# Quarter sums of the down-projection weights: made on VectorE and stored, or made in DRAM by copies and adding DMAs

## The chip, the cores and the metric

The kernel runs on one core of a Trainium2 chip. The metric is the device time of one execution in microseconds (us). Engines are named as in the profile: PE is TensorE (matmuls), PEld its weight loads, DVE is VectorE, ACT is ScalarE, POOL is GpSimd, SP is SyncE, which issues most DMAs here. DMAs that add to their destination are issued from POOL.

## The reference

It is a trunk of two layers over 512 tokens of width 1024, all in float32. Layer 0 mixes tokens with dilated banded attention in three head groups, layer 1 with forgetting attention over shared keys and values. After each mixer comes the same feed-forward part, which is where the change lies:

```python
def conv_ffn(xn, w_up, cw, cb, w_down):
    a = xn @ w_up                                   # 512x1024 @ 1024x5632
    T = a.shape[1]
    ap = jnp.pad(a, ((0, 0), (CONV_W - 1, 0), (0, 0)))
    a = sum(ap[:, j:j + T] * cw[j] for j in range(CONV_W)) + cb
    gate, val = jnp.split(a, 2, axis=-1)
    return (jax.nn.gelu(gate, approximate=True) * val) @ w_down   # 512x2816 @ 2816x1024
```

## The kernel before

Every product in float32 is made of three matmuls on high and low parts (`mm3`, L262): a float32 operand is cast to a rounded high part by ACT, and DVE subtracts that from the original to get the low part. Weights pass through the class `Weights` in a fixed list of pieces of 128 x 1024: `load` issues the DMA on SP (L46) into a tile `wraw` of the pool `t4` (10 buffers), `high` casts it on ACT (L54) into a tile of the pool `t8` (16 buffers), `low` subtracts on DVE (L62). `low_added` (L77) lets an adding DMA on POOL do that subtraction inside the core, from a negated copy that ACT makes; it is used at a few places. Tiles of a pool are handed out in turn, and whoever writes a tile first waits until the readers of its last use are done. The order of the instructions on each engine is the order in which the program writes them; nothing is reordered.

The feed-forward part of a layer (`ffn`) has two phases.

The up-projection runs over NF = 22 chunks `c` of 128 gate channels and the 128 value channels that belong to them. Chunks 6, 8, ..., 18 (`SEVEN`) use a scheme of seven products in place of eight (Strassen's, in Winograd's form); their weight sums are made by `seven_weights`, whose first DVE instructions are L656 and L657. While chunk `c` is multiplied, the weights of chunk `c + 2` are prepared and those of `c + 3` are loaded. `taps`, `glu` and `product` make the convolution, the gate and the product `hc`, and POOL stores `hc` to DRAM (`hD`, L608).

The down-projection (`down`) also uses seven products in place of eight, over ND = 11 pairs `j` of chunks. For it each pair of weight chunks needs sums of quarters. With the pair's two chunks of 128 rows, top and low, each cut into a left and a right half of 512 columns, the four sums are

- T1 = top right - top left, T3 = low right - top right, T2 = low right - T1, and a fourth, low left - T2.

`down_sums` makes them for a list of pairs: SP loads the two chunks (L553 to L555), DVE does four subtractions of 128 x 512 (L558 to L561), and the result is stored to the DRAM tensor `dT[l][j]` (L566), from where `Weights` loads it later as pieces of the down-projection, and `load_two` its last quarter. It is a generator, and each `next` on it takes one step: a load, and a sum and a store that lag behind. The places of these steps are written out by hand:

- during layer 0's attention, ten pairs of layer 0 in tiles of the pool `t8`, stored from SP, and two pairs of layer 1 in `t4`;
- during the projection of the shared keys and values, six pairs of layer 1, in `t4`, stored from POOL;
- at the end of each up-projection (from chunk NF - 3), the layer's last pair of layer 0 or 1 and one more of layer 1, in `t8`, stored from POOL.

On the activation side `pair_sums` makes the matching sums of token halves, and `combine_one` combines the partial products in the matmul banks.

Of the kernel before, what the change touches and what calls it, by code (L numbers as in the profile page):

```python
# [20 lines left out]
NF = DFF // 128  # L21
# [75 lines left out]
def trunk_kernel(ctx, tc, x, norm_gains, w_qkv_a, w_o_a, w_q_b, w_o_b, kv_norm, w_kvf, b_f,  # L97
# [11 lines left out]
    def t8(shape, dt=F32, name="t8"):  # L109
        return p8.tile(shape, dt, tag="t8", name=name)  # L110
# [429 lines left out]
        dve.tensor_copy(cp, pc)  # L540
        return cp

    def down_sums(pairs, place, queue, lag, behind):


        live, n = [], len(pairs)
        for i in range(n + lag + behind):
            if i < n:
                l, j = pairs[i]
                a, b = place()  # L550
                live.append((a, b))
                r = w_down[l][j * 256:j * 256 + 256, :].rearrange("(c p) d -> c p d", p=128)
                sp.dma_start(a, r[0])  # L553
                sp.dma_start(b[:, 0:512], r[1, :, 512:1024])
                sp.dma_start(b[:, 512:1024], r[1, :, 0:512])  # L555
            if 0 <= i - lag < n:
                a, b = live[i - lag]
                dve.tensor_tensor(a[:, 0:512], a[:, 512:1024], a[:, 0:512], ALU.subtract)  # L558
                dve.tensor_tensor(a[:, 512:1024], b[:, 0:512], a[:, 512:1024], ALU.subtract)
                dve.tensor_tensor(b[:, 0:512], b[:, 0:512], a[:, 0:512], ALU.subtract)  # L560
                dve.tensor_tensor(b[:, 512:1024], b[:, 512:1024], b[:, 0:512], ALU.subtract)  # L561
            i -= lag + behind
            if i >= 0:
                l, j = pairs[i]
                for q, t in enumerate(live[i]):
                    queue.dma_start(dT[l][j, :, q * 1024:q * 1024 + 1024], t)  # L566
            yield

    def in_one():
        t = t8([128, 2, 1024], name="dsums")  # L570
        return t[:, 0], t[:, 1]

    def in_two():
        return [t4([128, 1024], name="dsums") for _ in range(2)]

    def ffn(l, bd, cp, nxt, ahead):
        hD = tc.dram_tile([NF, 128, T], F32, name="hD")
# [117 lines left out]
        def pair_sums(j):  # L702

            pair_load(j + 1)
            k = acts[j]
            dve.tensor_tensor(k[:, s3_], k[:, a11], k[:, s1_], ALU.subtract)
            dve.tensor_tensor(k[:, s1_], k[:, s1_], k[:, s2_], ALU.add)
            dve.tensor_tensor(k[:, s2_], k[:, s1_], k[:, a11], ALU.subtract)
            pool.dma_start(sD[j], k[:, s2_])

        def pair_highs(j):
# [52 lines left out]
        def combine_one(bp):  # L764
            a, b, c, d = db[bp, 0], db[bp, 1], db[bp + 2, 0], db[bp + 2, 1]
            p1, u, u3 = (t2([128, 512], name="dsum") for _ in range(3))
            act.copy(p1, a)
            dve.tensor_tensor(u, b, p1, ALU.add)
            dve.tensor_tensor(c, c, u, ALU.add)
            act.copy(u3, c)  # L770
            dve.tensor_tensor(b, d, u, ALU.add)
            dve.tensor_tensor(d, d, u3, ALU.add)


        def p_11(j, bp):
# [98 lines left out]
        extra = sums_in()  # L874
        begun = None
        before = None
        for c in range(2, NF):
            if c == NF - 4:
                pair_load(0)
            if c == NF - 3:  # L880
                sums = down_sums([(l, ND - 1), (1, 8 + l)], in_one, pool, 1, 0)
                next(sums)
            steps = weights(c + 2) if c + 2 < NF else iter(())
            banks = [bank([128, T], name="up") for _ in range(2)]
            if c in SEVEN:
                w = halves.pop(c)
                W.n_get += 2
                x11, x21, x22 = [(xT[0][i], xT[1][i], s) for i, s in ((0, LO), (1, LO), (1, HI))]
                o1, o2, o3, o4 = banks[0][:, LO], banks[0][:, HI], banks[1][:, LO], banks[1][:, HI]
                s1, s12, s17 = (t2([128, 256], name="csum") for _ in range(3))  # L890

                def prod(o, a, x, start=False):
                    half_mm(o, w[a], x[0:2], x[2], start)

                prod(o1, "A11", x11, True)
                prod(o2, "S2", (*XB, HI))
                prod(o3, "S3", (*XA, HI), True)
                product()
                bb = taps(*before)
                act.copy(s1, o1)  # L900
                next(steps)
                dve.tensor_tensor(s12, o2, s1, ALU.add)
                dve.tensor_tensor(s17, o3, s1, ALU.add)
                glu(before[0], bb)
                prod(o1, "A12", x21)
                prod(o2, "S1", (*XA, LO))
                prod(o3, "A22", (*XB, LO))
                next(steps)
                next(steps, None)
                dve.tensor_tensor(o4, o2, s17, ALU.add)  # L910
                begun = W.get(), bank([128, T], name="up")
                up(*begun, range(4))
                prod(o2, "S4", x22)
                next(steps, None)
                dve.tensor_tensor(o3, o3, s12, ALU.add)
                next(steps, None)
                dve.tensor_tensor(o2, o2, s1, ALU.add)  # L917
            else:
                for s in range(2):
                    if s == 0 and begun:  # L920
                        w, banks[0] = begun
                        up(*begun, range(4, KD))
                        begun = None
                    else:
                        up(W.get(), banks[s], range(KD))
                    if c == NF - 2:
                        next(sums)
                    if s == 0 and before:
                        post(*before, (lambda: pair_lows(0)) if c == NF - 1 else None)
                        if c >= NF - 2:  # L930
                            pair_highs(c - NF + 2)
                            pair_sums(c - NF + 3)
                    next(steps, None)
                    next(extra, None)
            run(steps)
            before = c, banks
            if c == NF - 3:
                pair_sums(0)
# [249 lines left out]
    W.ahead = 4  # L1188
    W.split(6)
    qk_post(0, 3, qk_banks[3])  # L1190
    sums = down_sums([(1, 6), (1, 7)], in_two, sp, 1, 3)
    next(sums)
    reorder(2, 3)

    def wide_proj(g, name, post, between):

        banks = [bank([128, T], name=name) for _ in range(4)]
        for s in range(4):
            w = W.get()
            wh, wl = (t.rearrange("p (k c) -> p k c", k=2) for t in w)  # L1200
            for b in range(4):
                for k in range(2):
                    kc = 2 * s + k
                    ah, al = ax(g, b, kc)
                    mm3(banks[b], ah, al, wh[:, k, :], wl[:, k, :], kc == 0, kc == KD - 1)
                if s == 3:
                    post(g, b, banks[b])
            for f in between[s]:
                f()
            next(down0)  # L1210

    def v_post(g, b, o):
        if b == 0:
            for i in (1, 2):
# [1 line left out]
        act.copy(V[1][:, b, :], o[:, 0:256])  # L1216
        dve.tensor_copy(V[2][:, b, :], o[:, 256:512])

    down0 = down_sums([(0, j) for j in range(10)], in_one, sp, 1, 1)
    v_proj0([[L(qk_transpose, 0, 0), L(qk_transpose, 0, 1)],  # L1220
             [L(qk_transpose, 0, 2), L(qk_transpose, 0, 3), L(scores, 0, 0), L(scores, 0, 1), L(next, sums)]])
    wide_proj(1, "qk_ps", qk_post, [
        [L(p_transpose, 0, 0)],
        [L(scores, 0, 2), L(scores, 0, 3), L(p_transpose, 0, 1), L(next, sums)],
        [L(p_transpose, 0, 2), L(next, sums)],
        [stat_out, L(p_transpose, 0, 3), L(next, sums)]])
    wide_proj(2, "qk_ps", qk_post, [
        [L(qk_transpose, 1, 0), L(qk_transpose, 1, 1), L(next, sums)],
        [L(qk_transpose, 1, 2), L(scores, 1, 0), L(scores, 1, 1)],
        [L(qk_transpose, 1, 3), L(p_transpose, 1, 0)],  # L1230
        [L(scores, 1, 2), L(scores, 1, 3), L(p_transpose, 1, 1), stat_in]])
# [125 lines left out]
            Vt[hf] = t8([128, 4, 512], name=f"Vt{hf}")  # L1357
        (act.copy if b % 2 else dve.tensor_copy)(Vt[hf][:, b, :], o)

    down1 = down_sums([(1, j) for j in range(6)], in_two, pool, 1, 0)  # L1360
    first, second = bd2.order[:2], bd2.order[2:]
    bd2.norm(second[1])
    gate = gates()
# [17 lines left out]
            for bb in (first[second.index(blocks[0])], blocks[0]):  # L1381
                keep_values(0, bb, banks[bb])
    del wv
    next(down1)

    cks = {}

    def load_ck(j):
# [43 lines left out]
    for c in range(8):  # L1432
        keys(c)
        for kc in range(2 * c, min(2 * c + 2, KD)):
            if kc % 4 == 0:
                for part, name in zip(xTq, ("xqh", "xql")):
                    part.append(t8([128, 4, T], F32R, name=f"{name}{kc // 4}"))
            bd2.second(xTq, kc)
        if 1 <= c <= 5:
            next(gate)  # L1440
        if c in (0, 1):
            next(down1)
        if c == 6:
            sp.dma_start(cd, c8)
    cqp = bank([128, 4, 16], name="cq_ps")
# [6 lines left out]
    banks = [bank([128, 512], name="v_ps") for _ in range(4)]  # L1452
    for s in range(4):
        values(banks, value_weight(), s, range(4))
        next(down1, None)
        if s == 0:
            W.ahead = 2
            q_part(0, 0)
# [200 lines left out]
```

## Time and profile before

| | |
|---|---|
| time, median of 3 runs | 1128.06 us (1127.65 to 1130.12) |
| span of the profiled execution | 1125.8 us |
| time around that span | not recorded for this execution; the median of the runs is 2.3 us more than the span |
| busy PE | 1114.3 us, 99% of the span |
| busy DVE | 893.8 us, 79% |
| busy ACT | 616.5 us, 55% |
| busy POOL | 191.6 us, 17% |
| moved by DMA | 218.38 MB, mean 194 GB/s |

Busy time of PE is the union of its matmuls' spans, whose ends are modelled. A row of a group gives the line, the engine, the operation, what it writes and reads, how often, and its time; a number in square brackets at the end is the idle time of the engine just before it and what ended that. In rows of DMA queues, q1 holds what SP issued and q0 what POOL issued; their share is the time that their packets took, of 16 engines' time in the window. "To landing" is from issue to the last byte.

### The profile page before, as it was taken

Reading aid. Unit: us, or ns where it says so; the run is one execution under the profiler, and the core shown is the slowest. Engines: PE = TensorE matmul, PEld = TensorE weight load, DVE = VectorE, ACT = ScalarE, POOL = GpSimd, SP = SyncE. Lnnn points to the kernel's source line nnn. Section 1 sums busy time; section 2 is a strip of 40 time slices with the busy share of each in tenths; the row PEclk is TensorE's granted clock in tenths of the full one; section 3 lists DMA queues with packets and bytes.
Section 4 is the critical chain, followed back from the end, with each engine's and each line's share of the span. In section 5 each row is a group of like instructions: output and inputs, shape, how many; then the busy total and the mean of one; then the engine's idle time right before and its main releaser. Section 6 shows DMA issues by size and latency. Waiting matters only on the chain. (4 is left out here: it accounts for less than half of the span.)

```text
span 1125.8 us, 17268 instructions
## 1 busy us (share of the span) xinstructions
PE 1114.3 (99%) x6267; PEld 950.6 (84%) x6267; DVE 893.8 (79%) x1449; ACT 616.5 (55%) x1038; POOL 191.6 (17%) x291
## 2 busy tenths in 40 slices
PE   9999999999999999999999999999999999999997
PEld 6988889889899888888778888789989989988886
DVE  6668778888888689997588677847888788689894
ACT  5454565545444456576562588746444454456572
POOL 1832101200000121000000556600400000121000
PEclk9999999999999999999999999999999999999999
DMA  9469854333443699793447766473334343499861
GB/s 322 150 222 407 320 161 133 94 119 106 142 123 115 160 346 370 293 333 100 128 151 253 235 168 160 123 209 107 118 94 122 115 138 122 138 351 368 326 243 75
DMA packets 179471, 218.38 MB, mean 194 GB/s; under 512 B 11257, under 2 KB 131049, under 8 KB 179386
## 3 DMA queue, kind: packets, MB, share of 16 engines
q1 hardware_dynamic: 168634, 180.84, 49.0%
q0 software_dynamic: 10752, 36.45, 10.5%
q8 instruction: 49, 0.80, 0.3%
q14 instruction: 36, 0.29, 0.1%
HBM read 166.08 MB, written 39.63 MB: 183 GB/s over the span
## 5 line engine op out<-in xcount | busy, mean ns | idle before, releaser
L592 ACT ACTIVATE bb<-up,conv 128x512 f32<-128x512 f32 x80 | 60.6, 775 | 149.5 <-DVE up L917 76.2
L62 DVE TENSOR_TENSOR w<-wraw,w 128x1024 fp32r<-128x1024 f32 x96 | 123.0, 1312 | 22.1 <-ACT w L54 21.6
L54 ACT CAST w<-wraw 128x1024 fp32r<-128x1024 f32 x110 | 111.6, 1047 | 19.4 <-PE v_ps L264 11.6
L263 PE MATMUL acc<-w 128*128 128x512 f32 (+1 forms) x311 | 120.7, 388 | 1.1 <-DVE mix L310 1.1
L265 PE MATMUL acc<-w 128*128 128x512 f32 (+1 forms) x311 | 120.6, 388 | 0.0
L263 PE MATMUL up<-xch,w 128*128 128x512 f32 (+1 forms) x292 | 104.9, 359 | 0.0
L264 PE MATMUL up<-xcl,w 128*128 128x512 f32 (+1 forms) x292 | 104.9, 359 | 0.0
L263 PE MATMUL up<-xbh,w 128*128 128x512 f32 (+1 forms) x292 | 104.9, 359 | 0.0
L264 PE MATMUL up<-xbl,w 128*128 128x512 f32 (+1 forms) x292 | 104.9, 359 | 0.0
L265 PE MATMUL up<-xbh,w 128*128 128x512 f32 (+1 forms) x292 | 104.8, 359 | 0.0
L265 PE MATMUL up<-xch,w 128*128 128x512 f32 (+1 forms) x292 | 104.8, 359 | 0.0
L264 PE MATMUL acc<-w 128*128 128x512 f32 (+1 forms) x267 | 103.3, 387 | 0.0
L608 POOL DMA_DIRECT2D hD<-hc x42 | 24.2, 576 | 316.9 <-DVE hc L610 316.6
L263 PEld LDWEIGHTS acc<-w 128*128 128x128 f32 x311 | 58.4, 188 | 13.1 <-DVE mix L310 1.3
L265 PEld LDWEIGHTS acc<-w 128*128 128x128 f32 x311 | 58.4, 188 | 12.1 <-DVE w L720 0.3
L593 DVE SCALAR_TENSOR_TENSOR bb<-up,conv,bb 128x511 f32<-128x511 f32 x80 | 59.5, 744 | 7.7 <-ACT bb L592 7.7
L265 PE MATMUL up<-xsh,w 128*128 128x256 f32 x224 | 63.5, 283 | 0.0
L264 PE MATMUL up<-xsl,w 128*128 128x256 f32 x224 | 63.5, 283 | 0.0
L263 PE MATMUL up<-xsh,w 128*128 128x256 f32 x224 | 63.5, 283 | 0.0
L595 DVE SCALAR_TENSOR_TENSOR bb<-up,conv,bb 128x510 f32<-128x510 f32 x80 | 59.9, 749 | 2.8
L263 PEld LDWEIGHTS up<-xbh,w 128*128 128x128 f32 x292 | 55.1, 189 | 8.3
L263 PEld LDWEIGHTS up<-xch,w 128*128 128x128 f32 x292 | 55.1, 189 | 8.2
(303 smaller groups left out, 3040.7 us busy)
## 6 DMA issues: line engine op xcount, KB each, us to landing
wraw<-in_w_up_dram SPq DMA_DIRECT2D x88, 512.0 KB, 4.7
dT<-dsums SPq DMA_DIRECT2D x24, 512.0 KB, 6.5
dsums<-in_w_down_dram SPq DMA_DIRECT2D x22, 512.0 KB, 7.2
dsums<-in_w_down_dram SPq DMA_DIRECT2D x44, 256.0 KB, 6.6
hD<-hc POOLq DMA_DIRECT2D x44, 256.0 KB, 4.7
dact<-hD SPq DMA_DIRECT2D x44, 256.0 KB, 6.2
wraw<-dT SPq DMA_DIRECT2D x22, 512.0 KB, 9.9
wraw<-in_w_down_dram SPq DMA_DIRECT2D x22, 512.0 KB, 6.3
```

Source lines behind the costliest of these rows:

```text
L54: self.nc.scalar.copy(pair[:, 0], raw)
L62: self.nc.vector.tensor_tensor(pair[:, 1], raw, pair[:, 0].bitcast(F32), ALU.subtract)
L263: pe.matmul(o, ah, bh, start=first, stop=False, skip_group_check=shared)
L264: pe.matmul(o, ah, bl, start=False, stop=False, skip_group_check=shared)
L265: pe.matmul(o, al, bh, start=False, stop=last, skip_group_check=shared)
L592: act.activation(bb[:, s, :], ps, AF.Identity, bias=cp[:, 3, ch:ch + 1], scale=cp[:, 2, ch:ch + 1])
L593: dve.scalar_tensor_tensor(bb[:, s, 1:], ps[:, :T - 1], cp[:, 1, ch:ch + 1], bb[:, s, 1:], ALU.mult, ALU.add)
L595: dve.scalar_tensor_tensor(bb[:, s, 2:], ps[:, :T - 2], cp[:, 0, ch:ch + 1], bb[:, s, 2:], ALU.mult, ALU.add)
L608: pool.dma_start(hD[c - 1], hc.pop(c - 1))
```

## The change

`down_sums` no longer loads, computes and stores. It takes a layer `l` and makes all eleven pairs of that layer inside that layer's own up-projection, by DMAs that go from DRAM to DRAM. A pair passes six stages, one per chunk: `begin` copies the top chunk into the places of T1 and T3 (SP, 512 KB); `first` adds the top chunk's right half to the one and the low chunk's right half to the other (POOL, two adding DMAs of 256 KB); `again` copies T1 to the place of T2 (SP, 256 KB); `second` adds the low right quarter there (POOL); `again` copies T2 to the place of T4 (SP); `third` adds the low left quarter (POOL). At chunk `c = n + 2` stage `k` works on pair `n - k`, so the stages of six pairs run beside each other, from chunk 2 to chunk 17. In each chunk they are written ahead of that chunk's weight loads on SP and ahead of its store of `hc` on POOL.

A copy waits for the adds that made its source, an add for the copy that made its destination.

Since sums are now additions, T1 is top left + top right, T3 is top right + low right, T2 is T1 + low right and T4 is T2 + low left; the signs in `pair_sums` and `combine_one` are changed to suit. All steps of the old generator (in the attention, in the shared projection, at the end of the up-projection) are gone, and with them its tiles.

```diff
-    def down_sums(pairs, place, queue, lag, behind):
...
+    T1, T3, T2, T4 = (slice(i * 512, i * 512 + 512) for i in range(4))
+
+    def down_sums(l):
+
+        def quarters(j):
+            r = w_down[l][j * 256:j * 256 + 256, :].rearrange("(c p) d -> c p d", p=128)
+            return r[0], r[1]
+
+        def begin(j):
+            sp.dma_start(dT[l][j, :, 0:1024], quarters(j)[0])
+
+        def first(j):
+            top, low = quarters(j)
+            pool.dma_start(dT[l][j, :, T1], top[:, 512:1024], accum_op=ALU.add)
+            pool.dma_start(dT[l][j, :, T3], low[:, 512:1024], accum_op=ALU.add)
+
+        def again(dst, src):
+            return lambda j: sp.dma_start(dT[l][j, :, dst], dT[l][j, :, src])
+
+        def second(j):
+            pool.dma_start(dT[l][j, :, T2], quarters(j)[1][:, 512:1024], accum_op=ALU.add)
+
+        def third(j):
+            pool.dma_start(dT[l][j, :, T4], quarters(j)[1][:, 0:512], accum_op=ALU.add)
+
+        stages = (begin, first, again(T2, T1), second, again(T4, T2), third)
+        for n in range(ND + len(stages) - 1):
+            for k, f in enumerate(stages):
+                if 0 <= n - k < ND:
+                    f(n - k)
             yield
...
         def pair_sums(j):
             dve.tensor_tensor(k[:, s3_], k[:, a11], k[:, s1_], ALU.subtract)
-            dve.tensor_tensor(k[:, s1_], k[:, s1_], k[:, s2_], ALU.add)
-            dve.tensor_tensor(k[:, s2_], k[:, s1_], k[:, a11], ALU.subtract)
+            dve.tensor_tensor(k[:, s1_], k[:, s1_], k[:, s2_], ALU.subtract)
+            dve.tensor_tensor(k[:, s2_], k[:, a11], k[:, s1_], ALU.subtract)
...
         def combine_one(bp):
-            dve.tensor_tensor(u, b, p1, ALU.add)
-            dve.tensor_tensor(c, c, u, ALU.add)
+            dve.tensor_tensor(u, b, p1, ALU.subtract)
+            dve.tensor_tensor(c, c, u, ALU.subtract)
             act.copy(u3, c)
             dve.tensor_tensor(b, d, u, ALU.add)
-            dve.tensor_tensor(d, d, u3, ALU.add)
+            dve.tensor_tensor(d, d, u3, ALU.subtract)
...
+        sums = down_sums(l)
         for c in range(2, NF):
+            next(sums, None)
             if c == NF - 4:
                 pair_load(0)
-            if c == NF - 3:
-                sums = down_sums([(l, ND - 1), (1, 8 + l)], in_one, pool, 1, 0)
-                next(sums)
...
-                    if c == NF - 2:
-                        next(sums)
...
-    sums = down_sums([(1, 6), (1, 7)], in_two, sp, 1, 3)
-    down0 = down_sums([(0, j) for j in range(10)], in_one, sp, 1, 1)
-    down1 = down_sums([(1, j) for j in range(6)], in_two, pool, 1, 0)
...
```

(and every `next(sums)`, `next(down0)` and `next(down1)` in the attention and the shared projection is removed.)

More of the change, by code (lines that the diff above doesn't have):

```diff
@@ L541, in conv_columns @@
         return cp
-    def down_sums(pairs, place, queue, lag, behind):
[L546 to L566, printed above, removed]
-            yield
@@ L569, in in_one @@
[L569 to L574, printed above, removed]
+    T1, T3, T2, T4 = (slice(i * 512, i * 512 + 512) for i in range(4))
[20 more added lines that the diff above has]
+                    f(n - k)
+            yield
@@ L1190, in trunk_kernel @@
     qk_post(0, 3, qk_banks[3])
-    sums = down_sums([(1, 6), (1, 7)], in_two, sp, 1, 3)
-    next(sums)
     reorder(2, 3)
@@ L1209, in wide_proj @@
                 f()
-            next(down0)
     def v_post(g, b, o):
@@ L1217, in v_post @@
         dve.tensor_copy(V[2][:, b, :], o[:, 256:512])
-    down0 = down_sums([(0, j) for j in range(10)], in_one, sp, 1, 1)
     v_proj0([[L(qk_transpose, 0, 0), L(qk_transpose, 0, 1)],
-             [L(qk_transpose, 0, 2), L(qk_transpose, 0, 3), L(scores, 0, 0), L(scores, 0, 1), L(next, sums)]])
+             [L(qk_transpose, 0, 2), L(qk_transpose, 0, 3), L(scores, 0, 0), L(scores, 0, 1)]])
     wide_proj(1, "qk_ps", qk_post, [
         [L(p_transpose, 0, 0)],
-        [L(scores, 0, 2), L(scores, 0, 3), L(p_transpose, 0, 1), L(next, sums)],
-        [L(p_transpose, 0, 2), L(next, sums)],
-        [stat_out, L(p_transpose, 0, 3), L(next, sums)]])
+        [L(scores, 0, 2), L(scores, 0, 3), L(p_transpose, 0, 1)],
+        [L(p_transpose, 0, 2)],
+        [stat_out, L(p_transpose, 0, 3)]])
     wide_proj(2, "qk_ps", qk_post, [
-        [L(qk_transpose, 1, 0), L(qk_transpose, 1, 1), L(next, sums)],
+        [L(qk_transpose, 1, 0), L(qk_transpose, 1, 1)],
         [L(qk_transpose, 1, 2), L(scores, 1, 0), L(scores, 1, 1)],
@@ L1383, in trunk_kernel @@
     del wv
-    next(down1)
     cks = {}
@@ L1440, in trunk_kernel @@
             next(gate)
-        if c in (0, 1):
-            next(down1)
         if c == 6:
@@ L1454, in trunk_kernel @@
         values(banks, value_weight(), s, range(4))
-        next(down1, None)
         if s == 0:
```

## The prediction

> **What bounds the kernel now.** I read the page's head first, then the stretches, then what TensorE (PE) waited for.
>
> ```profile
> span 1125.8 us, 17268 instructions
> PE 1114.3 (99%) x6267; PEld 950.6 (84%) x6267; DVE 893.8 (79%) x1449; ACT 616.5 (55%) x1038; POOL 191.6 (17%) x291
> ```
> ```profile
> 0.00:25.00 25.00, 23.00 (x90) 15.62 (x91) 17.76 (x30) 15.25 (x26) 2.42 (x12) 1.00 0.96 329
> ...
> 100.00:125.00 25.00, 23.76 (x137) 19.65 (x136) 19.11 (x53) 11.60 (x41) 8.49 (x16) 1.00 1.03 404
> ...
> 289.00:331.00 42.00, 42.00 (x266) 38.17 (x265) 35.44 (x51) 19.58 (x27) 2.16 (x4) 1.00 0.42 127
> ...
> 1100.00:1125.00 25.00, 19.13 (x92) 15.86 (x90) 11.10 (x24) 7.42 (x21) 0.00 (x0) 0.97 0.22 84
> ```
>
> In the rows of stretches the columns are length, busy PE, weight loads, DVE, ACT, POOL, granted clock (1.00), DMA share and GB/s. PE is the bound: 11.5 us of the span are not busy, and of these 2.0 lie in the start, 5.9 in the end, 1.2 in 100 to 125 us. The up-projection (289 to 331 is a sample) has no idle PE at all, with DVE busy 35.44 of 42 us and the DMA engines at 0.42. So the change, which takes work from DVE, can win only where PE waited for DVE beside that work. The list of PE's waits has one such row:
>
> ```profile
> PE s_ps L1022 <- DVE qkT L998: 1.2, 1, 1.2
> ```
> ```profile
> 118.15 1.03 PE L995 MATMUL qkT_ps<-ident,qk 128*128 128x128 f32 x8
> 119.12 0.72 PE L1022 MATMUL s_ps<-qkT 64*128 64x128 f32 x8
> 121.08 1.08 PE L1022 MATMUL s_ps<-qkT 64*128 64x128 f32 x6 [1.24 <-DVE qkT L998]
> ```
> ```profile
> 119.20 1.23 DVE L62 TENSOR_TENSOR w<-wraw,w 128x1024 fp32r<-128x1024 f32 x1 [2.68 <-ACT w L54]
> 120.34 1.28 DVE L998 COPY qkT<-qkT_ps 128x512 f32<-128x512 f32 x2
> ```
> ```profile
> 118.12 1.05 ACT L54 CAST w<-wraw 128x1024 fp32r<-128x1024 f32 x1 [4.68 <-PE v_ps L264]
> ```
>
> Read backwards: PE waited 1.24 us for a copy on DVE (L998), which stood behind a weight's low part (L62), which waited for its cast on ACT (L54), which waited 4.68 us until PE had released a buffer of the pool of 16 big tiles. The quarter sums take tiles of that same pool.
>
> **What is removed.**
>
> ```profile
> L558 DVE TENSOR_TENSOR dsums<-dsums x22: 681/685/945, 52.3 to 997.1; 128x512 f32<-128x512 f32 x22
> ...
> L561 DVE TENSOR_TENSOR dsums<-dsums x22: 691/693/840, 54.4 to 999.6; 128x512 f32<-128x512 f32 x22
> ```
>
> 88 subtractions at 0.69 us are 61 us of DVE, and 66 loads and 44 stores. Off the path all but once: PE waits for DVE in no other row of weight. What it is worth: without sums in the big pool, the cast at 118.12 writes a tile released earlier, L62 comes ahead of L998, and the 1.24 us go. Ends: 0 if the cast is then held by its own load, and 1.3 us if every idle bit around there goes. I take 1.2, since the row names a buffer and not a load. Next late is PE itself. Taking the four extra pairs out of the ends of the up-projections frees queues where PE waits for nothing: 0.
>
> **Signs.** Four subtractions stand where additions stood and a fifth has its operands exchanged, in the same places and shapes: 0, no cover needed.
>
> **What is added.** All falls into the up-projection, over chunks 2 to 17 of each layer. A pair costs one copy of 512 KB and two of 256 KB on SP, and four adding DMAs of 256 KB on POOL. No DMA of before reads and writes DRAM, so the price comes from the nearest rows: large loads and stores of the sums between DRAM and the core's memory (75 to 125 us), and one adding DMA inside the core (704.8 to 710.5 us).
>
> ```profile
> q1 hardware_dynamic: 7597, 19.83, 103.0%
> q14 instruction: 3, 0.02, 0.1%
> ```
> ```profile
> q0 software_dynamic: 150, 0.52, 48.2%
> ```
> ```profile
> L77 POOL DMA_DIRECT2D w<-wraw x14: 835/893/932, 382.4 to 991.8; - x14
> ```
>
> A copy: 103% of 50 us for 19.83 MB, 2.60 us of all 16 engines per MB, so 1.36 us for 512 KB and 0.68 for 256 KB. An add: 48.2% of 5.7 us is 2.75 us for 512 KB, 1.37 for 256 KB. A pair: 1.36 + 2 x 0.68 + 4 x 1.37 = 8.2 us. What is there already, and how fast the chunks go (247 to 331 us, eight chunks):
>
> ```profile
> q1 hardware_dynamic: 16627, 8.38, 34.7%
> q0 software_dynamic: 610, 2.03, 5.9%
> ...
> wraw<-in_w_up_dram SPq DMA_DIRECT2D x16, 512.0 KB, 4.0
> hD<-hc POOLq DMA_DIRECT2D x8, 256.0 KB, 4.6
> ```
> ```profile
> L656 DVE TENSOR_TENSOR wsum<-wraw x6: 682/682/683, 252.9 to 358.0; 128x512 f32<-128x512 f32 x6
> ```
>
> L656 comes once in two chunks: 105.1/5 = 21.0 us, 10.5 a chunk. The old load is 40.6% of 84 us, 4.26 us a chunk. With all six stages running a chunk wants 8.2 + 4.26 = 12.5 us of DMA in 10.5. That holds for six chunks (12 us over), and the chunk on either side is 0.6 over: a backlog of 13.2 us at its worst, which drains afterwards (11 x 8.2 + 20 x 4.26 = 175 us of 210).
>
> Who waits for that backlog? Nobody reads the sums before the down-projection, but the weight loads share the engines, and on SP they stand behind the copies, which wait for adds. The tightest load is the second tile of a seven-product chunk:
>
> ```profile
> 342.40 0.37 SPq L46 DMA_DIRECT2D wraw<-in_w_up_dram  x1
> ```
> ```profile
> 358.04 0.68 DVE L656 TENSOR_TENSOR wsum<-wraw 128x512 f32<-128x512 f32 x1
> ```
> ```profile
> SPq L46 <- DVE w L663: 46.8, 6, 8.3
> ```
>
> It is issued when its buffer comes free (last row, so it cannot go earlier), 15.6 us ahead of its use, and lands in 4.0: 11.6 us of cover. Behind it DVE has 6.6 us free in 42, 3.3 in two chunks: 14.9 in all. Against that stand, at most, the whole 13.2, and if the two queues share the engines evenly, only SP's part: its own 3.64 + 2.72 = 6.4 a chunk against half of 10.5, so 1.15 x 6 = 7 us. Both are covered; I take cost 0, with 1.7 us to spare in the worse reading.
>
> POOL gets four adds of 0.89 us before each chunk's store of the gated product (L608), 3.6 us of the 10.5, and waits for copies. Behind it the store comes late; its buffer is one of 8, of which two chunks take five, so it has some three chunks, 31 us, less 4.6 to land: 0 up to there. POOL's two sums of the inputs (L627) come ahead of the first add. SP issues three more DMAs a chunk at 0.37 us, 1.1 us, inside the cover above.
>
> **Sum.** -1.2 + 0 + 0. The profiled span is 1125.8; the median of the runs is 1128.06, 2.3 more, and I keep that distance: 1126.8.
>
> **Rivals.**
> B, the weight loads land too late (slower). Place: L656 and the cast beside it, once in two chunks, where 15.6 us now lie between issue and use. For it: rows of 375 to 400 us, where adds, sums and loads ran together at full DMA engines, and a load took 13.2 us, not 4:
>
> ```profile
> w<-wraw POOLq DMA_DIRECT2D x4, 512.0 KB, 9.0
> ...
> wraw<-dT SPq DMA_DIRECT2D x2, 512.0 KB, 13.2
> ```
>
> Against it: 13.2 is still under 15.6. It decides from a lateness of 11.6 to 14.9 us. Without DVE's reserve the 13.2 cost 1.6 a layer, 3 us; with prices 15% up the backlog is about 23 and leaves 8 a layer, 16 us. Between, with the 1.2 gained: 1130 to 1143, say 1134.
>
> C, DRAM to DRAM pays the load and the store one after the other (slower). Then a copy costs double, an add 1.37 + 0.68. SP's part is 3.64 + 5.44 a chunk, 3.8 over its half in nine chunks, 34 - 14.9 = 20 a layer: 1167. If all the backlog (about 61 a layer) fell on the loads: 46 a layer, 1219. Against it: loads and stores in one queue cost 2.60 us per MB in the row above, whichever way they go, and an engine that reads and writes at once would pay once.
> The Trainium skill, page "DMA: Bandwidth & Descriptors", section "Latency and other measured facts", has copies between HBM tensors at 207 to 214 GB/s per direction; as an estimate from it a pair's 1.05 MB of copies take 4.9 us, which would lead to C. The page "Collectives: The Full Stack", section "The bandwidth ceiling: the fold count and why AG ≠ RS ≠ AR", has HBM copies at about 31 GB/s per engine and adding at half, because an add reads two sources; by that DRAM is no dearer and the forecast stands, and the rows above agree on the half (5.3 against 2.6 us per MB). No row here decides between the pages.
>
> D, faster by more than 2.3 us. It would need idle PE that the rows don't show; in 25 to 125 us, where most of the sums run, PE's idle time is 1.3. 1125.5 or less.
>
> E, the gap stays, since the cast would be held by its load: 1128.0, inside the forecast's class.
>
> **How the numbers follow.** 0.2% is 2.3 us, about what a measurement of this kernel tells from no change. The forecast with E 0.47, B 0.25, C 0.20, D 0.08. Faster: D and a little of the forecast, 0.12. Same: the rest of the forecast and B's lower edge, 0.40. Slower: 0.48. The time is the likeliest case's, 1126.8, whose own range is 1125 to 1129. The range goes from 1124.5 to 1170: it takes in B and the lower end of C, and leaves out C's dear half (0.12) and little below.
>
> **What would show it.** Right: no idle PE before L1022 near 120 us; in the up-projection DMA share near 1 in its middle, weight loads landing in 6 to 14 us, PE still without idle time; no dsums rows on DVE. Wrong: ACT or DVE waiting for wraw in the up-projection and PE idle there in steps of two chunks (B), or DMA share at 1 through the whole of it and into the down-projection, with copies of 512 KB well over 1.36 us of the engines (C).

## The result, and the profile after

The changed kernel takes 1179.87 us (median; 1179.21 to 1182.0), against 1129.09 us for the kernel before on the same chip: a ratio of 1.0449, 95% interval 1.0432 to 1.0466, 50.8 us slower. The forecast was 1126.8 us, with a range up to 1170. The profiled execution took 1179.37 us, 1177.6 of them span, 51.8 us more than the span of before.

The head of the page of the changed kernel:

```profile
span 1177.6 us, 17212 instructions
PE 1127.1 (96%) x6267; PEld 962.5 (82%) x6267; DVE 836.2 (71%) x1361; ACT 618.0 (52%) x1038; POOL 250.0 (21%) x359
PEclk9999999999889999999999999999999889999999
```

Two things stand in it. PE was busy for 12.8 us more than the 1114.3 of before with the same 6267 matmuls, and its granted clock, 1.00 in the prediction's rows of before up to the last stretch, has two dents (an 8 is 0.8). The rest of the 51.8 us is PE standing still. The list of waits says where (us in total, times, longest):

```profile
PE up L263 <- DVE csum L893: 38.1, 7, 9.3
DVE wsum L648 <- DMA wraw<-in_w_up_dram: 39.1, 7, 9.4
```

L648 is the first sum of weight quarters of a seven-product chunk (L656 of before), L893 the first sum of a finished product. Both are on DVE, and L893 stands behind L648 with one more weight sum (L649) between them. So a weight tile came late, DVE waited for it at L648, and PE waited for the L893 behind it: seven times, 38.1 us in all, nearly the whole of the 39.1 us that DVE waited. These 38.1 of idle PE and 12.8 of slower PE make 50.9; waits of 1 to 2 us in the second attention and the gap that went (below) nearly cancel out.

The stretches, with the columns of the prediction (length, busy PE, weight loads, DVE, ACT, POOL, granted clock, DMA share, GB/s):

```profile
100.00:125.00 25.00, 25.00 (x144) 20.81 (x143) 9.71 (x39) 13.36 (x43) 6.33 (x16) 1.00 0.00 1
...
289.00:331.00 42.00, 34.13 (x198) 30.64 (x197) 26.57 (x37) 14.88 (x20) 9.20 (x12) 0.92 1.05 221
```

The attention (first row) has lost its idle time, as forecast: PE 25.00 where before had 23.76, and the row of the wait at L1022 is gone. The up-projection (second row), where before had 42.00 us of PE in 42, a clock of 1.00 and a DMA share of 0.42, has PE at 34.13, the clock at 0.92 and the DMA engines full. This is the DMA view of 100 us of it (225 to 325): packets, MB and share of the 16 engines by queue, then KB and median us from issue to landing.

```profile
q0 software_dynamic: 4183, 8.44, 51.5%
q1 hardware_dynamic: 15996, 13.52, 50.6%
...
wraw<-in_w_up_dram SPq DMA_DIRECT2D x14, 512.0 KB, 23.8
dT<-in_w_down_dram POOLq DMA_DIRECT2D x27, 256.0 KB, 10.9
dT<-in_w_down_dram SPq DMA_DIRECT2D x7, 512.0 KB, 20.2
```

q1 is SP's queue (weight loads and copies), q0 POOL's (adds, and the stores of gated products). Each took half of the engines, with nothing left over. Weight loads landed 23.8 us after their issue; in the same stage of before it was 4.0. SP's own queue in this stage:

```profile
280.99 3.89 SPq L46 DMA_DIRECT2D wraw<-in_w_up_dram  x1
284.93 15.21 SPq L552 DMA_DIRECT2D dT<-in_w_down_dram  x1
```
```profile
305.43 0.69 DVE L648 TENSOR_TENSOR wsum<-wraw 128x512 f32<-128x512 f32 x1 [7.18 <-DMA wraw<-in_w_up_dram]
```

The load issued at 280.99 is the one that L648 waited for at 305.43. It took 24.3 us to land. DVE was ready for it 7.18 us before 305.43, at 298.25, which is 17.3 us after the issue. So this load was not issued late (before had 15.6 us at this place); it landed late.

The issue of one copy held SP for 15.21 us, where an issue took 0.37 in before. Full engines alone do not do that. In a run below (row_loads_sp: weight loads in pieces of 4 KB) the two queues were as full over the same 100 us, and the same copies were issued in 0.5 to 1.62 us:

```profile
q0 software_dynamic: 4339, 8.72, 51.3%
q1 hardware_dynamic: 5240, 15.39, 50.5%
...
L552 SPq DMA_DIRECT2D dT<-in_w_down_dram x7: 497/502/1623, 237.6 to 303.7; - x7
```

SP's queue moved 5240 packets there and 15996 here, so the number of packets that stand in the queue may be what holds SP; no run tests that alone.

### The profile page after: what moved, and what is told of

It is laid out like the page before. It is cut to its first block, busy times and chain, and to the rows that moved or that the text cites. A ratio compares the mean times of both kernels' runs of the same rounds, so it can differ in the third digit from the quotient of the medians.

```text
span 1177.6 us, 17212 instructions
## 1 busy us (share of the span) xinstructions
PE 1127.1 (96%) x6267; PEld 962.5 (82%) x6267; DVE 836.2 (71%) x1361; ACT 618.0 (52%) x1038; POOL 250.0 (21%) x359
## 4 chain that ended last, share of the span: by engine, by line
PE 79%; DMA 12%; DVE 4%; SPq 2%; ACT 1%; issue 1%; POOL 0%; DVEq 0%; POOLq 0%; ACTq 0%
DMA wraw<-in_w_up_dram 9%; PE up L263 9%; PE up L264 8%; PE up L265 8%; PE acc L263 8%; PE acc L265 8%; PE acc L264 8%; PE v_ps L263 2%; PE v_ps L265 2%; PE v_ps L264 2%; PE qk_ps L264 2%; PE qk_ps L263 2%; PE qk_ps L265 2%; PE s_ps L1476 1%; PE first L265 1%; PE first L263 1%
## 5 line engine op out<-in xcount | busy, mean ns | idle before, releaser
L263 PE MATMUL up<-xch,w 128*128 128x512 f32 (+1 forms) x292 | 107.0, 366 | 21.9 <-DVE csum L893 21.9
L263 PE MATMUL up<-xbh,w 128*128 128x512 f32 (+1 forms) x292 | 106.9, 366 | 16.2 <-DVE csum L893 16.2
L265 PE MATMUL up<-xch,w 128*128 128x512 f32 (+1 forms) x292 | 106.3, 364 | 0.0
L265 PE MATMUL up<-xbh,w 128*128 128x512 f32 (+1 forms) x292 | 106.3, 364 | 0.0
L263 PEld LDWEIGHTS up<-xbh,w 128*128 128x128 f32 x292 | 56.7, 194 | 25.1 <-DVE csum L893 16.8
L263 PEld LDWEIGHTS acc<-w 128*128 128x128 f32 x311 | 58.4, 188 | 13.1 <-DVE mix L310 1.3
L263 PE MATMUL up<-xsh,w 128*128 128x256 f32 x224 | 65.8, 294 | 0.0
L265 PE MATMUL up<-xsh,w 128*128 128x256 f32 x224 | 65.4, 292 | 0.0
L264 PEld LDWEIGHTS up<-xcl,w 128*128 128x128 f32 x292 | 56.9, 195 | 8.1
L265 PEld LDWEIGHTS up<-xbh,w 128*128 128x128 f32 x292 | 56.8, 194 | 8.2
## 6 DMA issues: line engine op xcount, KB each, us to landing
dT<-in_w_down_dram POOLq DMA_DIRECT2D x88, 256.0 KB, 10.5
dT<-in_w_down_dram SPq DMA_DIRECT2D x22, 512.0 KB, 13.2
```

The source lines that it names most:

```text
L263: pe.matmul(o, ah, bh, start=first, stop=False, skip_group_check=shared)
L264: pe.matmul(o, ah, bl, start=False, stop=False, skip_group_check=shared)
L265: pe.matmul(o, al, bh, start=False, stop=last, skip_group_check=shared)
```

## The experiments

The theories: **E**, the 16 DMA engines have more to do in the up-projection than fits. **Q**, the order of SP's queue: weight loads stand behind copies, and those wait for adds. **P**, the two queues are served piece by piece in turn (a piece is a packet of the profile), so that the big pieces of one crowd out the small pieces of the other. **G**, for the part that was removed: all it is worth is the gap before L1022.

### The sums thinned out, or cheaper

Half the rate: a pair begins in every second chunk, eight to a layer. (Its stages follow one another by one chunk, as in the changed kernel, and not by two as the expectation has it.)

```diff
-        for n in range(ND + len(stages) - 1):
+        for n in range(20):
             for k, f in enumerate(stages):
-                if 0 <= n - k < ND:
-                    f(n - k)
+                if n >= k and (n - k) % 2 == 0 and (n - k) // 2 < 8:
+                    f((n - k) // 2)
```

> Eight pairs of each layer instead of eleven, a new one begun in every second chunk and each of its stages two chunks after the one before; the last three pairs read a top chunk of the down-projection's weights in place of their sums, so the output is another. By the prices of the prediction DMA has 4.1 + 4.26 = 8.4 us to do in a chunk of 10.5. Theory E: no backlog, the time is 1126.8 to 1131 us. Theory Q: each copy was made possible a whole chunk earlier, so its wait is gone too: 1127 to 1131 as well, unless SP's blocked issue of copies is a cost of each copy by itself, then half of the loss stays, 1150.

Plain writes in place of adds:

```diff
-            pool.dma_start(dT[l][j, :, T1], top[:, 512:1024], accum_op=ALU.add)
+            pool.dma_start(dT[l][j, :, T1], top[:, 512:1024])
...
```

> The four adding DMAs of a pair write without adding: the same issues, the same order of waits between SP and POOL, the same addresses written, but one source read less; what is in the tiles is no sum, so the output is another. A pair's DMA work goes from 8.2 to 1.36 + 6 x 0.68 = 5.4 us, so a chunk wants 9.7 us of 10.5. Theory E: the backlog is gone, 1127 to 1133 us. Theory Q: the copies still wait for POOL's DMAs and the loads for the copies: 1150 to 1175 us.

Measured: 1127.29 us for half the rate, ratio 0.9979 (0.9969 to 0.9989), and 1127.27 us for plain writes, 0.9977 (0.9965 to 0.9988). PE is busy for 1113.3 and 1114.2 us, and no wait of the up-projection is left. Both are as E has it: 8.4 or 9.7 us of DMA in a chunk of 10.5 cost nothing, 12.5 cost 51. Q, which with plain writes expected 1150 or more, falls in this form: the copies still waited for POOL's DMAs, and nothing was late. But plain writes also shorten these waits (13.1 us at L560, against 30.1 in the changed kernel), so the stronger test of Q is the last experiment below.

### No sums at all, none in the attention, and the signs

```diff
-                                  (raw[:, 512:1024], dT[l][j, :, 0:512])])
+                                  (raw[:, 512:1024], w_down[l][j * 256:j * 256 + 128, 512:1024])])
...
-            next(sums, None)
```

> No sums are made at all: neither on DVE nor by DMAs; the tiles that would hold them are loaded from a top chunk of the down-projection's weights, so the output is another. It shows what the removed part of the change is worth without the added one. Both theories: the 1.24 us before L1022 of the kernel before are gone, PE has no idle time in the up-projections, PE busy is back at 1114 us and the time is 1126.8 us, 0.1% under before. If the freed DVE and buffers were worth more, it would be under 1125.5.

The kernel before, without its ten sums in the attention:

```diff
-    down0 = down_sums([(0, j) for j in range(10)], in_one, sp, 1, 1)
+    down0 = iter(())
...
```

> The kernel before without the ten sums that run during the attention (layer 0, pairs 0 to 9, in tiles of the pool of 16); its other twelve pairs stay on DVE; the ten pairs' tiles are loaded from a top chunk of the weights, so the output is another. Theory G (all that the removed half of the change is worth is the one gap before L1022, which these ten sums cause): the ratio is that of the kernel with no sums at all, 0.9977, and the gap is gone. Rival: freeing DVE and the buffers is worth something in both layers: the ratio lies between 0.998 and 1.000.

The kernel before with the new signs:

```diff
-                dve.tensor_tensor(a[:, 0:512], a[:, 512:1024], a[:, 0:512], ALU.subtract)
+                dve.tensor_tensor(a[:, 0:512], a[:, 512:1024], a[:, 0:512], ALU.add)
...
```

> The kernel before with its sums on DVE in the attention and behind it, but with the new signs throughout (additions where the four sums of weight quarters stood as subtractions, and the four turned operations of the down-projection). All theories: same shapes, same engines, no difference: ratio 1.000 within 0.0015, and the idle time of PE before L1022 stays at 1.2 us.

Measured: no sums 1127.05 us, ratio 0.9977 (0.9967 to 0.9987); none in the attention 1127.08 us, 0.9978 (0.9970 to 0.9987); the signs 1130.49 us, 1.0002 (0.9993 to 1.0011). So signs cost nothing, and G holds as far as the intervals tell: the ten sums in the attention give all that the removed half is worth, and for the other twelve there is nothing left that could be told from noise (each ratio is known to about 0.001). But 0.0023 of some 1129.5 us is 2.6 us, and the gap has 1.24. The run of the signs, which has that gap too, shows the rest. Its wait, its stretch behind the gap and the slow part of that stretch, then the same stretch of the profiled execution of before:

```profile
PE s_ps L1022 <- DVE qkT L998: 1.2, 1, 1.2
...
122.00:130.00 8.00, 8.00 (x33) 6.43 (x32) 5.50 (x21) 4.61 (x18) 0.00 (x0) 0.79 1.00 399
123.20:126.60 3.40, 3.40 (x10) 2.61 (x9) 3.08 (x8) 3.40 (x14) 0.00 (x0) 0.50 1.04 414
```
```profile
122.00:130.00 8.00, 7.95 (x51) 6.40 (x50) 6.09 (x28) 5.02 (x21) 0.00 (x0) 1.00 1.02 400
```

After the same gap the granted clock is 0.79 over 8 us in one execution (0.50 for 3.4 us, 1.00 for the rest) and 1.00 in the other; 0.21 of 8 us is 1.7. The spans differ by 2.9 us (1128.7 and 1125.8) and PE's busy time by 1.8 (1116.1 and 1114.3). Executions of the kernel before lie between 1127.1 and 1132.5 us, those without the ten sums between 1126.4 and 1128.9. The profiled execution of before was one without the slow stretch. Of three profiled executions with the gap (before, signs and the kernel of the next experiment) two have the slow stretch behind it; of the eleven without the gap none has it. And of the 57 executions of before that were timed beside these runs, 20 have a mean clock of 0.996 or 0.997 and a median of 1131.0 us, the other 37 a higher clock and a median of 1129.0.

### What a standstill of PE costs

The kernel before, with DVE held up in one chunk of each layer and no DMA added:

```diff
             act.copy(w[0][:, 0], r0)
+            if c == 12:
+                for _ in range(19):
+                    dve.tensor_tensor(sa[:, 0:512], a11, a21, ALU.subtract)
             dve.tensor_tensor(sa[:, 0:512], a11, a21, ALU.subtract)
```

> The kernel before, with 19 more subtractions of 0.68 us on DVE ahead of the sums of one chunk (12) in each layer: 13 us, of which DVE's reserve takes 3 to 6, so PE stands still for 7 to 10 us twice, with no DMA added. If a standstill by itself lowers the granted clock behind it, as the rows after the waits of the changed kernel have it (0.80 to 0.93), PE's busy time grows by 4 to 8 us over before's 1114.3, and the time is 1146 to 1156 us. If the clock fell there because of the DMA load, PE's busy time stays within 1 us, and the time is 1142 to 1148 us.

Measured: 1162.45 us, ratio 1.0286 (1.0266 to 1.0306), PE busy 1121.0 us. PE's wait (L905 of this kernel is L893 of the changed one), the stretch behind the gap in the attention, and the group with the 38 added subtractions:

```profile
PE up L263 <- DVE csum L905: 27.1, 2, 13.6
...
122.00:130.00 8.00, 8.00 (x32) 6.33 (x32) 5.38 (x19) 4.62 (x18) 0.00 (x0) 0.79 1.01 383
```
```profile
L658 DVE TENSOR_TENSOR wsum<-wraw 128x512 f32<-128x512 f32 x38 | 26.3, 692 | 1.2
```

26.3 us of DVE cost 27.1 us of PE: DVE has no reserve at this place, none of the 3 to 6 us per standstill that I expected. And PE's busy time grew by 6.7 us over the 1114.3 of before. Of these, 1.7 are the slow stretch behind the gap in the attention (0.79 above), which the profiled execution of before did not have; against the run of the signs, which had it (1116.1), the growth is 4.9 us, some 2.5 for each standstill. The stretches during and behind the first standstill, then the same of the changed kernel:

```profile
298.00:312.00 14.00, 0.71 (x6) 0.50 (x5) 13.39 (x21) 1.16 (x2) 0.00 (x0) 0.60 0.03 9
312.00:317.00 5.00, 4.74 (x22) 4.74 (x23) 3.06 (x5) 2.62 (x3) 0.00 (x0) 0.50 0.02 5
317.00:322.00 5.00, 5.00 (x30) 4.51 (x30) 2.71 (x4) 0.00 (x0) 0.00 (x0) 0.92 0.33 100
```
```profile
299.00:307.00 8.00, 1.09 (x10) 0.88 (x8) 1.57 (x4) 1.64 (x3) 0.00 (x0) 0.84 1.06 307
307.00:312.00 5.00, 4.89 (x25) 4.89 (x26) 2.90 (x5) 2.62 (x3) 3.94 (x5) 0.58 1.07 285
312.00:317.00 5.00, 5.00 (x33) 4.51 (x32) 3.02 (x4) 0.00 (x0) 1.58 (x2) 1.00 1.12 194
```

In the 5 us behind a standstill the clock is 0.50 with the DMA engines idle (0.02) and 0.58 with them full (1.07). It is the standstill that slows PE, not the DMA load. Not every standstill does so. In the changed kernel the clock fell to 0.50 behind six of the seven, and behind the one of 3.5 us at 893 us it stayed at 1.00:

```profile
895.00:905.00 10.00, 8.45 (x59) 7.96 (x60) 7.37 (x11) 2.52 (x3) 3.93 (x5) 1.00 1.04 228
```

The Trainium skill, page "TensorE: Matmul & The Clock Gate", section "HAM oscillation — how this bites in real kernels", has the clock fall after idle gaps of over about 3.4 us. The half clock behind the long gaps agrees with it; the gap of 1.2 us before L1022 should then be harmless, and in the run of the signs it was not.

### Who issues, and in what pieces

All of a pair's DMAs on POOL, so that SP has the weight loads alone:

```diff
-            sp.dma_start(dT[l][j, :, 0:1024], quarters(j)[0])
+            pool.dma_start(dT[l][j, :, 0:1024], quarters(j)[0])
...
-            return lambda j: sp.dma_start(dT[l][j, :, dst], dT[l][j, :, src])
+            return lambda j: pool.dma_start(dT[l][j, :, dst], dT[l][j, :, src])
```

> The copies between DRAM tiles are issued by POOL, in order with the adds, and SP has the weight loads alone; the bytes are the same. Theory Q (the loads stand behind copies in SP's queue, and those behind adds): the loads of seven-product chunks land within 11 us of their issue, PE has under 5 us of idle time behind L893, and the time is 1127 to 1133 us. Theory E (the 16 DMA engines have more to do than fits, whoever issues it): the loads still land 20 us after issue and the time stays at 1165 to 1180 us. If both count, something between, say 1145.

Measured: 1201.65 us, ratio 1.0637 (1.0595 to 1.0679), 22 us worse than the changed kernel: outside what Q and E allowed. Its DMA view (225 to 325 us) and its waits:

```profile
q0 software_dynamic: 5800, 14.30, 69.1%
q1 hardware_dynamic: 13470, 6.79, 26.3%
```
```profile
PE up L263 <- DVE csum L893: 72.7, 5, 25.7
DVE wsum L648 <- DMA wraw<-in_w_up_dram: 65.0, 5, 18.8
```

In before SP's queue takes 34.7% of the engines in this stage, all of it weight loads; here the loads got 26.3%, though SP had nothing else to do. POOL's pieces are of 2 and 4 KB, those of a weight load of 512 bytes. That gave theory P, and two tests of it, from both sides. The sums in pieces of 512 bytes (blocks of 128 columns interleaved, the down-projection's loads to match):

```diff
+    def quarter(l, j, i):
+        h = i // 2 * 1024
+        return dT[l][j, :, h:h + 1024].rearrange("p (k t c) -> p k t c", t=2, c=128)[:, :, i % 2]
...
-            pool.dma_start(dT[l][j, :, T1], top[:, 512:1024], accum_op=ALU.add)
+            pool.dma_start(quarter(l, j, T1), bits(top[:, 512:1024]), accum_op=ALU.add)
...
```

> As copies_on_pool (all of a pair's DMAs on POOL, weight loads alone on SP), but the sums are laid out in blocks of 128 columns, so that every copy and add moves pieces of 512 bytes, as the weight loads do, in place of 2 and 4 KB. The same bytes in four times as many pieces can only make more work for the DMA engines. Theory E (only the sum of the engines' work counts): the time goes above 1201 us, to some 1230. Theory P (the engines serve the two queues piece by piece in turn, so that big pieces crowd out small ones): the weight loads get about half of the engines instead of 26%, land within 15 us, PE's idle time behind the sums of L893 falls from 73 us to under 15, and the time is 1130 to 1150 us; the sums themselves take longer.

The weight loads in pieces of 4 KB:

```diff
-            add_cols(w_up[l], c * 128)
-            add_cols(w_up[l], DFF + c * 128)
+            add(lambda raw, c=c: [(raw, w_up[l][c % 8 * 128:c % 8 * 128 + 128, 0:1024])])
+            add(lambda raw, c=c: [(raw, w_up[l][c % 8 * 128:c % 8 * 128 + 128, DFF:DFF + 1024])])
```

> As copies_on_pool, but a weight load of the up-projection reads 128 whole pieces of 4 KB (rows of other columns, so the output is another) instead of 1024 pieces of 512 bytes. The loads' work falls from 4.26 to about 3.3 us a chunk, the total from 12.5 to 11.6 of 10.5. Theory E: the backlog falls a little, 1165 to 1190 us. Theory P: the loads get a share as large as the sums', land in under 8 us, and the time is 1126 to 1131 us.

Both edits again, with the copies on SP as in the changed kernel:

> The changed kernel with the sums laid out in blocks of 128 columns, so that copies (SP) and adds (POOL) move pieces of 512 bytes. Theory E: more work for the engines than in the changed kernel, so over 1180 us, about 1210. Theory P: adds of 512 bytes no longer crowd out the loads; SP's queue gets its share and the time is 1128 to 1150 us, although the engines do more work.

> The changed kernel with its copies on SP and its adds on POOL, but the weight loads of the up-projection read 128 pieces of 4 KB each (rows of other columns; the output is another) in place of 1024 of 512 bytes. Theory E (only the sum of the engines' work counts): the total falls by 0.9 us of 12.5 a chunk, and at most half of the loss goes: 1150 to 1165 us. Theory P (the queues are served piece by piece in turn): SP's queue now has pieces as large as the adds' and gets its work done in time, loads land within 15 us: 1127 to 1133 us.

Measured (us, ratio to the kernel before, 95% interval):

| sums / weight loads in pieces of | copies on SP | copies on POOL |
|---|---|---|
| 2 and 4 KB / 512 B | 1179.87, 1.0449 (1.0432 to 1.0466) | 1201.65, 1.0637 (1.0595 to 1.0679) |
| 512 B (copies on POOL: 4 KB) / 512 B | 1164.56, 1.0313 (1.0292 to 1.0333) | 1141.11, 1.0100 (1.0084 to 1.0116) |
| 2 and 4 KB / 4 KB | 1157.97, 1.0241 (1.0224 to 1.0259) | 1142.47, 1.0114 (1.0097 to 1.0130) |

In the traces of the second row the adds move packets of 512 bytes, as meant, and so do the copies where SP issues them; the copies that POOL issues still go in packets of 4 KB.

Right column: with adds in small pieces the engines had more work (64 ns at the least for an add's packet of 512 bytes, against 44 for a quarter of one of 2 KB) and the kernel was 60 us faster. That is P against E, where E expected 1230. The DMA view of that run, 225 to 325 us:

```profile
q0 software_dynamic: 17071, 16.42, 83.0%
q1 hardware_dynamic: 17182, 8.67, 35.6%
```

The loads had 35.6% of the engines instead of 26.3, and SP's queue moved 8.67 MB, near the 9.47 of the kernel without sums. POOL's queue was no weaker rival than before: it had 83.0% instead of 69.1. (The shares add up to more than 100%, so packets overlap in time.) POOL also took longer to issue an add, up to 2.89 us against 1.80; but with loads of 4 KB, where its longest is 1.80 again, no load was late either. That the two queues moved about as many packets is no rule of sharing: SP's had nearly all that it wanted, and 2268 of POOL's packets are of 4 KB. Where the sizes differed most, the queues were equal neither in count (13470 to 5800) nor in time (26.3 to 69.1%). So these runs show that the queue of small pieces loses against the one of large pieces, and by what rule they share stays open. The Trainium skill, page "DMA: Bandwidth & Descriptors", section "Queues, rings and completion order", says that an engine goes round the queues packet by packet, a packet there being some 9 to 17 descriptors; the counts above neither show such turns nor exclude them.

With 4 KB loads and the copies on POOL no load was late any more, but 1142.47 is not the 1126 to 1131 that P expected. The waits name the rest:

```profile
PE up L263 <- DVE csum L894: 10.0, 3, 4.9
```
```profile
DVE csum L894 <- DMA hD<-hc: 20.1, 4, 7.6
```

The store of the gated product stood behind seven sum DMAs in POOL's queue, and its buffer, which the sums at L893 and L894 need, came free too late. With the sums in small pieces the same row stands (the line is L905 there), and in the changed kernel none like it:

```profile
DVE csum L905 <- DMA hD<-hc: 13.5, 3, 7.0
```

Left column: both edits help, but P's 1127 to 1133 and 1128 to 1150 are missed by far; with 4 KB loads the time is what E expected. There the loads share SP's queue with the copies. SP's wait for the adds, in the last row's kernel with copies on SP (row_loads_sp) and then in the kernel of the next experiment:

```profile
SPq L560 <- DMA dT<-in_w_down_dram: 153.7, 34, 11.2
```
```profile
SPq L560 <- DMA dT<-in_w_down_dram: 126.3, 21, 29.3
```

In the first, SP stood 153.7 us at L560, copies waiting for adds, with weight loads behind them. That fits Q in a kernel whose engines are full, but no run separates it there from SP's queue simply having more to move. Moving the copies off SP's queue saves 15 to 23 us in the two lower rows, and costs 22 in the first, where POOL's pieces are the larger ones throughout.

### All sums, with room for them

```diff
-    def down_sums(l):
+    def down_sums(l, pairs, every):
...
-        sums = down_sums(l)
+        sums = down_sums(l, range(8), 2)
...
+    early = down_sums(0, range(8, ND), 1)
...
+            next(early, None)
```

> All sums are made, by the same copies and adds, but eight pairs of a layer begin in every second chunk of the up-projection, and the last three are made earlier, where the DMA engines have room: in the attention for layer 0, beside the keys of the second attention for layer 1. The output is the reference's. Theories E and P: 8.4 us of DMA in a chunk of 10.5, no late load: 1126.8 to 1128.5 us, at or under the kernel before. Theory Q (order of SP's queue): 1140 us or more, since the copies still wait for adds of the chunk before and the loads stand behind them.

Measured: 1126.93 us, ratio 0.9977 (0.9967 to 0.9987), under both kernels and level with the kernel that makes no sums. The second row above is this kernel's: SP waited 126.3 us at L560, in the same order of the queue, and yet its stretch has no idle PE:

```profile
275.00:300.00 25.00, 25.00 (x167) 23.08 (x166) 20.34 (x29) 12.39 (x17) 4.51 (x6) 1.00 1.08 211
```

So Q costs nothing by itself. A DMA share of 1.08 in this row is no harm either, as the loads of 225 to 325 us landed in 8.7 us:

```profile
wraw<-in_w_up_dram SPq DMA_DIRECT2D x19, 512.0 KB, 8.7
```

What counts is whether the queue falls behind over several chunks.

## Why the prediction was wrong

**The gap before L1022: right in place, short in size.** It went. Its worth is 2.6 us instead of 1.2. In some executions a slow stretch of 1.7 us follows it (0.79 over 8 us), which the profiled one did not have, so that it costs up to 2.9; how often it does was not counted exactly.

**Signs: right**, 1.0002.

**The prices of copies and adds: right while one queue works.** In the packet records of the changed kernel's trace (225 to 325 us) the undisturbed packets of each kind take 84 ns for 2 KB and 159 for 4 KB of a copy, 176 for 2 KB of an add, 27 for 512 bytes of a weight load. A copy of 512 KB (128 packets on 16 engines) is then 1.27 us, forecast 1.36; one of 256 KB 0.67, forecast 0.68; an add 1.41, forecast 1.37. So the copies between DRAM tiles cost what the loads and stores of before cost per byte, an undisturbed copy does not pay twice as rival C had it, and an add takes 2.1 times as long as a copy. Of the two pages of the Trainium skill weighed there, "Collectives: The Full Stack" (section "The bandwidth ceiling: the fold count and why AG ≠ RS ≠ AR"), which has adds at half the rate, agrees. Prices from rows with one queue at work were, however, put into a stage where two fill the engines: between 225 and 325 us the means are 123, 227, 232 and 31 ns. At the undisturbed prices the packets of these 100 us would take 79 us of the engines; they took 102. Why the copies' means rise by 1.4 to 1.5 and the loads' by 1.15 no run shows. A chunk's DMA is then, on SP, 2048 x 31 + 128 x 227 + 256 x 123 = 7.8 us of the 16 engines where the forecast had 6.4, and on POOL 512 x 232 and the store, 8.1 us.

**"14.9 in all", cost 0: the step that failed**, in both of its sides. On the side of the load, the sentence "only SP's part ... 1.15 x 6 = 7 us" had the right share (each queue got half, 50.6 and 51.5%) and the wrong work: 7.8 against half of 10.5 is 2.5 short in a chunk, 15 in six chunks, and loads landed 20 us later than in before. The worse reading, the whole backlog of 13.2, grows with the same prices too: 15.9 against 10.5 is 5.4 in a chunk, 32 in six. On the side of the cover, the 3.3 us of DVE do not exist there: the added 26.3 us of DVE came through to PE whole, and of the 39.1 us that DVE waited in the changed kernel 38.1 did, since the sum that PE waits for stands behind the one that waits for the load. The cover was the 11.6 us alone. 20 late less 11.6 is 8.4 us a standstill, a rough figure from medians; the load followed above took 24.3 us with 17.3 until its use, 7.0 late. The trace has seven standstills, of 5.4 us on average and 9.3 at most.

**Rival B was right in mechanism and place** (L648 and L893, steps of two chunks), with 0.25 for it, and short in price: 8 us a layer at most, against 19 of idle PE and 6.4 of slower PE. The second term, the clock behind the standstills, was in no part of the forecast; it is a quarter of the loss.

**POOL, SP's issue, the stores: half right.** The adds' issue cost nothing and no store was late in the changed kernel. SP's three DMAs more, put at 0.37 us each, took up to 15.21 us each in the full stage.

**D and E: no.** The gap went, so E is out. The 2.6 us that the removed half is worth are a little over D's 2.3, but they come from the gap and the clock behind it, not from idle time elsewhere: nothing clear of noise came from freeing DVE or the buffers beyond the ten sums (0.9977 with no sums, 0.9978 without those of the attention).

## What to carry to other kernels

Where a DMA stage becomes full, price packets by rows in which the queues already compete, count each queue's work against its share, and look at the size of the pieces: a queue of small pieces loses its engines to one of large pieces. A late transfer's cover ends at the first instruction in line that waits for it, together with all that stands behind it on that engine, so idle time elsewhere on the engine is no reserve. Reckon with a slow stretch behind a new standstill of PE: 2.5 us for one of 13.6 here, 1.8 on average for the seven of the changed kernel (12.8 us in all).

## What was not expected of the hardware

- The granted clock behind a standstill: 0.50 to 0.58 for about 5 us behind long ones, 0.50 for 3.4 us in two of three executions behind a gap of 1.2 us, and 1.00 behind one of 3.5 us.
- Packets of 2 KB that add in DRAM take 176 ns undisturbed and 232 on average in the full stage, copies of 2 KB 84 and 123.
- An issue on SP took up to 15.21 us in the full stage, and at most 1.62 for the same copies with the engines as full but the weight loads in pieces of 4 KB.
- Of two queues in competition the one with small pieces loses: 26.3% of the engines for pieces of 512 bytes against 2 and 4 KB, 35.6% once the adds are of 512 bytes too. By what rule they share stays open.
